# Convolution first stage by partition halves with paired row tiles, and earlier PSUM copies in fc1

## The chip, the cores and the metric

The kernel runs on one core of one Trainium2 chip. The metric is the device time of one execution in microseconds. A core has five engines that run side by side, each with a queue that it works off in order: TensorE (PE, with PEld for its weight loads), VectorE (DVE), ScalarE (ACT), GpSimd (POOL) and SyncE (SP), which here mostly issues DMAs. TensorE writes its results to PSUM, which has eight banks of 512 f32 per partition; DVE and ACT read them from there.

## The reference

One layer of a hybrid block on x of 2048 positions by 1024 channels, in f32:

```python
h = rmsnorm(x, g_mix); p = h @ w_in            # 512 Fourier columns, 3 x 512 Hyena columns
y_f = rmsnorm(fourier_mix(p[:, :512]), g_fourier)
u = short_conv(p[:, 512:], conv_w, conv_b); x1, x2, z = split(u)
for n, gate in enumerate((x1, x2)):            # two long convolutions, by FFT
    y = irfft(rfft(z, 4096) * k_freq[:, n], 4096)[:2048]
    z = gate * (y + z * long_d[n])
x = x + concat(y_f, rmsnorm(z, g_hyena)) @ w_out
x = x + square(relu(rmsnorm(x, g_mlp) @ w_fc1)) @ w_fc2
out = rmsnorm(x, g_final)
```

The two convolutions have 512 channels each; fc1 is 1024 by 4096 and fc2 4096 by 1024.

## The kernel before

The stages follow one another: input projection, short convolution, Fourier mix and filters (to about 618 us of the profiled execution), the two long convolutions (`hyena`, to about 845), output projection (`project_out`), fc1 (about 1045 to 1675) and fc2.

**The convolutions.** `hyena` works in eight blocks: `n` (first or second convolution) by `ct` (four groups of 128 channels). The transform over 4096 points is done in two matmul stages with a turn between them:

- `first(c)` (L712 to L719), for c = 0 to 7, takes 16 channels. Its two matmuls (L718) multiply `zz`, 128 partitions by 16 positions by 16 channels = 256 columns, by the two matrices `e1[:, sp, :]`. The table builds `e1z` so that matrix `sp` is nonzero only in partitions 64 sp to 64 sp + 63: each matmul has 128 rows, of which 64 are zeros. The two results fill the two halves of one PSUM bank, and `turned` (L446) transposes the bank on DVE into `G`.
- `second(q)` (L721 to L735), for q = 0 to 7, does four matmuls of `G` (L725, so it needs all eight turns), then ACT, DVE and POOL multiply by the filter's spectrum.
- `inverse(q)` (L736 to L742) does four matmuls (L741) and an ACT copy into `V`; `turn` transposes `V` into `W` on DVE.
- `gate(q)` (L749 to L757) does two matmuls (L754), each with 64 columns of weights, into the two partition halves of a bank, and DVE multiplies by the gate.

The loop below `blocks` runs block i with q = 0 to 7: `second(q)` of block i, at q = 1 four `gate` of block i - 2, then `inverse`, then `first` of block i + 1 as the table `FIRSTS` says: two at q = 0, two at q = 1, one each at q = 2 to 5. So the first stage of one block is woven into the block before it; only block 0's stands alone, ahead of the loop.

**fc1.** `fc1` multiplies by a Strassen-like scheme: each of the 32 steps does seven products (m1 to m7) of twelve 128x512 matmuls (in mm3, three for each of four slices: high by high, high by low, low by high). Several products add up in one bank `pu`: m1, then m6, then m7, then m4 of the same step. After m1, m6 and m7 the bank's state is copied out by `keep` on ACT (L1142 to L1145; `km1`, `ku2`, `ku3`), and the next product may not add to the bank before that copy is done. A step i issues m1, then m4 and m3 of step i - 1 among its own m2, m6, m5, m7. Tokens are taken in two blocks of 1024: steps 0 to 15 and 16 to 31. In step 15, right after the last use of each product's token operand, the operand of the second block is loaded into the same tile and split into a high part (ACT, L184) and a low part (DVE, L185).

**What sets the order.** Each engine's queue is made by the tile framework when the kernel is built: it takes the instructions by priority, which is their place in the program text, but passes over one that it expects to be still waiting. Under `tc.high_priority(offset=400)` an instruction counts as if it stood 400 places earlier. The framework adds the semaphore waits; two accesses to one bank of a tile are ordered even where their columns differ.

Of the kernel before, what the change touches and what calls it, by code (L numbers as in the profile page):

```python
# [10 lines left out]
F32 = mybir.dt.float32  # L11
# [118 lines left out]
P = 128  # L130
# [6 lines left out]
def hybrid_block(ctx: ExitStack, tc: tile.TileContext, A, out):  # L137
    nc = tc.nc
# [24 lines left out]
    small = ctx.enter_context(tc.tile_pool(name="small", bufs=8))  # L163
# [4 lines left out]
    def pa(nm):  # L168
        return ps.tile([P, 512], F32, tag="a", name=nm, bufs=8)
# [11 lines left out]
    def split(hi, lo, src, scale=None, eng=None):  # L181

        if scale is None:
            nc.scalar.copy(hi, src)  # L184
            (eng or nc.vector).tensor_sub(lo, src, hi)  # L185
        else:
            nc.scalar.mul(hi, src, scale)  # L187
            nc.vector.scalar_tensor_tensor(out=lo, in0=src, scalar=scale, in1=hi, op0=ALU.mult, op1=ALU.subtract)  # L188
# [255 lines left out]
    def turned(dst, c, src):  # L444

        nc.vector.transpose(dst.rearrange("p c f e -> p c e f")[:, 8 * c : 8 * c + 8], src)  # L446
# [230 lines left out]
    def hyena(hp, wp, rp, zz, e1, b1, f2, a2, work):  # L677
# [3 lines left out]
        def big(nm):  # L681
            return (rp if nm == "W" else wp).tile([P, 64, 32, 2], F32, tag=nm, name=nm, bufs=1 if nm == "W" else 2)

        class Block:
# [24 lines left out]
                        nc.gpsimd.memset(ks[h : h + 1, 1, 0, :], 0.0)  # L709
                return ks  # L710

            def first(self, c):  # L712
                if c == 0:
                    self.G = big("G")
                p = pa("pz1")
                lo = 128 * self.ct + 16 * c
                for sp in range(2):
                    nc.tensor.matmul(p[:, 256 * sp : 256 * sp + 256], lhsT=e1[:, sp, :], rhs=zz[:, :, lo : lo + 16], start=True, stop=True)  # L718
                turned(self.G, c, p.rearrange("p (l c e) -> p c e l", c=8, e=2))  # L719

            def second(self, q):  # L721
                ks = self.ahead.pop(q) if q in self.ahead else self.spectrum(q)
# [36 lines left out]
        LAG = 3  # L759
        TURNS = ((0,), (1,), (2, 3), (4, 5), (6, 7))  # L760
        LAST = ((0,), (1, 2), (3, 4), (5, 6), (7,))
        FIRSTS = ((0, 1), (2, 3), (4,), (5,), (6,), (7,), (), ())
        blocks = [Block(n, ct) for n in range(2) for ct in range(4)]
        for k in range(4):
            blocks[0].ahead[k] = blocks[0].spectrum(k)

            nc.sync.dma_start(a2[:, 8 * k : 8 * k + 8], A["a2"][:, 8 * k : 8 * k + 8])
        for c in range(8):
            blocks[0].first(c)
        for i in range(8):  # L770
            cur, old, older, new = (blocks[j] if 0 <= j < 8 else None for j in (i, i - 1, i - 2, i + 1))
            for q in range(8):
# [28 lines left out]
                if new:  # L801
                    for c in FIRSTS[q]:
                        new.first(c)
# [247 lines left out]
    def fc1_load(b, blk, n):  # L1051

        nc.sync.dma_start(b[n][1].bitcast(F32), bd[blk][n])
# [14 lines left out]
    def fc1_sums(eng, wa, wb, s):  # L1068
        a11, a12, a21, a22 = wa[:, 0:4], wa[:, 4:8], wb[:, 0:4], wb[:, 4:8]
        eng.tensor_add(s[0], a21, a22)  # L1070
        eng.tensor_sub(s[1], s[0], a11)
        eng.tensor_sub(s[2], a11, a21)
        eng.tensor_sub(s[3], a12, s[1])
# [16 lines left out]
    def fc1_store(c, queue, f, n):  # L1090
        blk, f = divmod(f, 16)
        queue.dma_start(ad[blk][n][f], c)
# [23 lines left out]
    def fc1(mp, rp, zp, b, first, following, begun):  # L1116


        def weights(wa, wb, step):
            a = {}  # L1120
            a11, a12, a22 = wa[:, 0:4], wa[:, 4:8], wb[:, 4:8]

            def put(n, src, eng=None):
                a[n] = [mp.tile([P, 4, P], FR, tag=f"a{h}", name=f"a{h}{n}", bufs=9) for h in "hl"]
                split(*a[n], src, None, eng)

            if step == 0:
                s = None, None, a11, a12
            else:
                if step > 1:  # L1130
                    put("m1", a11)
                    put("m2", a12, nc.gpsimd)
                s = [mp.tile([P, 4, P], F32, tag="sa", name=f"s{j}", bufs=4) for j in range(4)]
                fc1_sums(nc.gpsimd, wa, wb, s)
                put("m6", s[1])
                put("m5", s[0], nc.gpsimd)
            put("m7", s[2])
            put("m3", s[3], nc.gpsimd)
            put("m4", a22, nc.gpsimd)
            return a  # L1140

        def keep(p, nm):  # L1142
            t = mp.tile([P, 512], F32, tag="keep", name=nm, bufs=4)
            nc.scalar.copy(t, p)  # L1144
            return t  # L1145

        def activate(f, half, h, p, other):
            c = mp.tile([P, 512], F32, tag="c", name="c", bufs=11)
            n = {(0, 0): "m1", (1, 0): "m2", (1, 1): "m4"}.get((half, h))
            fc1_activate(c, p, other, nc.sync if f < 30 else nc.scalar, f, n)  # L1150
            acts[f, half, h] = c

        def sums(f):

            a11, a12, a21, a22 = (acts.pop((f, *k)) for k in ((0, 0), (1, 0), (0, 1), (1, 1)))
            s1, s2, s4 = (mp.tile([P, 512], F32, tag="c", name=n, bufs=11) for n in ("s1", "s2", "s4"))
            nc.vector.tensor_add(s1, a21, a22)
            nc.vector.tensor_sub(s2, s1, a11)
            nc.vector.tensor_sub(a21, a11, a21)
            nc.vector.tensor_sub(s4, a12, s2)  # L1160
            for n, t in (("m6", s2), ("m5", s1), ("m3", s4), ("m7", a21)):
                fc1_store(t, nc.sync if f < 30 else nc.scalar, f, n)

        acts = {}

        mp.tile([P, 512], F32, tag="c", name="c", bufs=11)
        mp.tile([P, 512], F32, tag="keep", name="keep", bufs=4)
        for h in "hl":  # L1170
            mp.tile([P, 4, P], FR, tag=f"a{h}", name=f"a{h}", bufs=9)
        mp.tile([P, 4, P], F32, tag="sa", name="sa", bufs=4)
        b["m4"] = [mp.tile([P, 4, 512], FR, tag=f"b{h}m4", name=f"b{h}m4") for h in "hl"]
        with tc.high_priority(offset=700):
            fc1_load(b, 0, "m4")
            old, nxt = None, weights(*first, 0)
        with tc.high_priority(offset=200):
            for n in ("m7", "m4", "m3"):
                fc1_split(b, n)
        acts[0, 0, 0] = mp.tile([P, 512], F32, tag="c", name="c0", bufs=11)  # L1180
        nc.sync.dma_start(acts[0, 0, 0], ad[0]["m1"][0])
        for i in range(33):
            def use(p, a, n, start, step):
                if n in a:
                    fc1_product(p, a[n], b[n], start)
                if step == 15:
                    fc1_tokens(b, 1, n)

            if i < 32:
                a = nxt  # L1190
                if i < 31:
                    nxt = weights(*(fc1_weights(rp, (i + 1) % 16, 1 - i % 2) if i else following), i + 1)
                pu, pm = (pa("p1u"), pa("p1m")) if i > 1 else begun[3 * i : 3 * i + 2]
                use(pu, a, "m1", True, i)
                if i:
                    m1 = keep(pu, "km1")
            if old:
                use(old["u"], old["a"], "m4", False, i - 1)
                activate(i - 1, 1, 0, old["u"], None)
            if i < 32:  # L1200
                use(pm, a, "m2", True, i)
                if i:
                    activate(i, 0, 0, pm, m1)
            if old:
                use(old["v"], old["a"], "m3", False, i - 1)
                activate(i - 1, 0, 1, old["v"], old["u2"])
                sums(i - 1)
            if i < 32:
                use(pu, a, "m6", False, i)
                with tc.high_priority(offset=0 if i else 400):  # L1210
                    u2 = keep(pu, "ku2")
                pv = pa("p1v") if i else begun[2]
                use(pv, a, "m5", True, i)
                use(pu, a, "m7", False, i)
                u3 = keep(pu, "ku3")
                activate(i, 1, 1, pv, u3)
                old = {"u": pu, "v": pv, "a": a, "u2": u2}

        zf = zp.tile([P, 8, 2, 512], FR, tag="zz", name="zf")
        fc2_begun = {}  # L1220
        for i, n in enumerate(("m1", "m2")):
            parts = []
            for j, v in enumerate(fc2_rows(0, n, 0)):
                t = rp[:, 2 * i + j, :].rearrange("p (f c) -> p f c", f=2)
                nc.sync.dma_start(t, v)
                parts.append((zf[:, 4 * i + 2 * j], zf[:, 4 * i + 2 * j + 1]))
                split(*parts[j], t)
            fc2_begun[n] = [pa("p2" + "um"[i]) for _ in range(4)]
            for j, p in enumerate(fc2_begun[n]):
                fc2_product(p, j, *parts, True)  # L1230
        return fc2_begun
# [205 lines left out]
    zz, = zzs  # L1437
    b1 = load(tabs.enter_context(pool("tabs2", "right")), "b1", [P, P], A["b1"])
    with pool("raws") as rp:
        with pool("wts") as wp:  # L1440
# [7 lines left out]
            with pool("op") as op:  # L1448
                first = project_out(op, work, raws, b)
# [58 lines left out]
```

## Time and profile before

| | us |
|---|---|
| median of 3 runs (2299.31 to 2301.06) | 2300.55 |
| the profiled execution | 2297.96 |
| its span | 2296.2 |
| PE busy, in matmuls | 2237.3 |
| DVE busy | 1509.3 |
| ACT busy | 1110.5 |
| POOL busy | 824.8 |

In the profile, a row of the timeline is start, length, engine, line, operation, out<-in, form, count, and in brackets the idle time before it and what ended it. A count x8 merges eight instructions in a row; the length runs from the first one's start to the last one's end. A matmul's own length includes the time until its result is written, so that lengths of neighbours overlap: what it costs PE is the distance from one start to the next. A row of a tile's list is engine, operation, tile, count, then the shortest, median and longest duration in ns. "f32" also stands for the fp32r operands of mm3 in matmul rows.

### The profile page before, as it was taken

What the parts mean: (1) busy time and instruction counts of PE and PEld (TensorE: products, weight loads), DVE (VectorE), ACT (ScalarE), POOL (GpSimd) and SP (SyncE); (2) the same over time, 40 slices, a digit from 0 to 9 for tenths busy, and PEclk for the clock granted to TensorE, in tenths of its full rate; (3) what the DMA queues carried; (4) which work ended last, traced back from release to release, by engine and by line L of the source; (5) the groups of instructions that cost most, each with busy time, mean ns of one, the idle gap of its engine ahead of it and who ended that gap; (6) DMA issues with size and microseconds to landing.
All of it is one profiled execution on the core that took longest, in us unless ns stands there. A gap on an engine that the chain in (4) does not pass through costs nothing.

```text
span 2296.2 us, 31043 instructions
## 1 busy us (share of the span) xinstructions
PE 2237.3 (97%) x11025; PEld 1853.2 (81%) x11025; DVE 1509.3 (66%) x2258; ACT 1110.5 (48%) x1849; POOL 824.8 (36%) x623
## 2 busy tenths in 40 slices
PE   8999999999899989998999989999999999999998
PEld 6887788799788858887888878888888888888886
DVE  6999776778678774458444465444476666866667
ACT  6555211566366564456555565555543333533333
POOL 3344323677376611146555556555400000000000
PEclk9999999999999999999999999999999999999999
DMA  8545886689987766667444475444489766866631
GB/s 266 181 140 187 329 303 245 226 292 319 324 274 208 216 195 187 178 202 234 158 149 150 150 250 162 152 152 151 142 315 346 245 190 195 299 195 193 192 119 74
DMA packets 298797, 487.31 MB, mean 212 GB/s; under 512 B 17477, under 2 KB 141711, under 8 KB 294417
## 3 DMA queue, kind: packets, MB, share of 16 engines
q1 hardware_dynamic: 292977, 470.91, 62.5%
q10 hardware_dynamic: 5664, 14.41, 1.8%
q8 instruction: 87, 1.43, 0.3%
q14 instruction: 69, 0.57, 0.1%
HBM read 314.64 MB, written 169.05 MB: 211 GB/s over the span
## 4 chain that ended last, share of the span: by engine, by line
PE 78%; DVE 4%; DMA 3%; ACT 2%; issue 1%; POOL 1%; SPq 0%; ACTq 0%; DVEq 0%; POOLq 0%
PE p2u L193 5%; PE p2u L192 5%; PE p2u L194 5%; PE p1u L192 5%; PE p1u L194 5%; PE p1u L193 5%; PE p2v L193 3%; PE p2v L192 3%; PE p2v L194 3%; PE pu L194 2%; PE pu L193 2%; PE pu L192 2%; PE p1v L192 2%; PE p1v L194 2%; PE p1v L193 2%; PE po L192 2%
## 5 line engine op out<-in xcount | busy, mean ns | idle before, releaser
L184 ACT CAST qahm<-ra 128x1024 fp32r<-128x1024 f32 x110 | 115.9, 1053 | 344.5 <-PE p2u L193 172.0
L185 DVE TENSOR_TENSOR qalm<-ra,qahm 128x1024 fp32r<-128x1024 f32 x110 | 134.7, 1225 | 153.8 <-ACT qahm L184 151.8
L1282 POOL TENSOR_TENSOR acc<-acc,gfin 128x512 f32<-128x512 f32 x4 | 5.1, 1276 | 631.9 <-DMA out<-acc 624.7
L192 PE MATMUL pu<-wh,xh 128*128 128x512 f32 x512 | 204.4, 400 | 4.8 <-ACT wh L187 3.6
L193 PE MATMUL pu<-wl,xh 128*128 128x512 f32 x512 | 201.7, 394 | 3.6 <-DVE wl L188 3.5
L194 PE MATMUL pu<-wh,xl 128*128 128x512 f32 x512 | 201.2, 393 | 0.2 <-DVE xl L185 0.2
L193 PE MATMUL p2u<-qblm,qahm 128*128 128x512 f32 x504 | 196.1, 389 | 0.0
L192 PE MATMUL p2u<-qbhm,qahm 128*128 128x512 f32 x504 | 195.8, 389 | 0.0
L194 PE MATMUL p2u<-qbhm,qalm 128*128 128x512 f32 x504 | 195.8, 389 | 0.0
L185 DVE TENSOR_TENSOR qblm<-rb,qbhm 128x1024 fp32r<-128x1024 f32 x110 | 134.1, 1219 | 3.5 <-ACT qbhm L184 3.0
L383 POOL TENSOR_TENSOR acc<-acc,cw 128x512 f32<-128x512 f32 x45 | 59.9, 1331 | 201.6 <-DVE acc L360 200.3
L184 ACT CAST ahm<-s 128x512 fp32r<-128x512 f32 x124 | 76.6, 621 | 100.6 <-PE p1v L193 55.3
L185 POOL TENSOR_TENSOR alm<-W,ahm 128x512 fp32r<-128x512 f32 x63 | 85.5, 1357 | 99.7 <-ACT ahm L184 93.1
L193 PEld LDWEIGHTS pu<-wl,xh 128*128 128x128 f32 x512 | 97.3, 190 | 25.6 <-DVE wl L188 4.9
L184 ACT CAST qbhm<-rb 128x1024 fp32r<-128x1024 f32 x110 | 115.3, 1048 | 5.4 <-DMA rb<-in_w_fc 4.2
L192 PEld LDWEIGHTS pu<-wh,xh 128*128 128x128 f32 x512 | 97.1, 190 | 25.7 <-ACT wh L187 4.0
L194 PEld LDWEIGHTS pu<-wh,xl 128*128 128x128 f32 x512 | 97.2, 190 | 21.3 <-DVE xl L185 1.1
L192 PEld LDWEIGHTS p2u<-qbhm,qahm 128*128 128x128 f32 x504 | 94.6, 188 | 20.2 <-issue 0.3
L193 PEld LDWEIGHTS p2u<-qblm,qahm 128*128 128x128 f32 x504 | 94.6, 188 | 19.6
L194 PEld LDWEIGHTS p2u<-qbhm,qalm 128*128 128x128 f32 x504 | 94.6, 188 | 19.5
L192 PE MATMUL p1u<-bm,ahm 128*128 128x512 f32 x252 | 100.2, 398 | 8.1 <-ACT ku L1144 8.1
L184 ACT CAST ahm<-W 128x512 fp32r<-128x512 f32 x94 | 57.5, 615 | 100.9 <-PE p1u L193 98.8
(397 smaller groups left out, 6429.5 us busy)
## 6 DMA issues: line engine op xcount, KB each, us to landing
W<-in_w_fc SPq DMA_DIRECT2D x66, 512.0 KB
spec<-ks SPq DMA_DIRECT2D x32, 1024.0 KB
ks<-spec SPq DMA_DIRECT2D x64, 512.0 KB
rb<-td SPq DMA_DIRECT2D x64, 512.0 KB
ra<-a1m SPq DMA_DIRECT2D x56, 512.0 KB
ra<-a0m SPq DMA_DIRECT2D x54, 512.0 KB
rb<-in_w_fc SPq DMA_DIRECT2D x46, 512.0 KB
f<-in_w_fc SPq DMA_DIRECT2D x16, 1024.0 KB
```

The source lines that it names most:

```text
L184: nc.scalar.copy(hi, src)
L185: (eng or nc.vector).tensor_sub(lo, src, hi)
L192: nc.tensor.matmul(o, lhsT=lh, rhs=rh, start=start, stop=False, skip_group_check=more)
L193: nc.tensor.matmul(o, lhsT=lh, rhs=rl, start=False, stop=False, skip_group_check=more)
L194: nc.tensor.matmul(o, lhsT=ll, rhs=rh, start=False, stop=stop, skip_group_check=more)
L383: nc.gpsimd.tensor_add(m1, m1, cw[:, 3, :])
L1282: nc.gpsimd.tensor_mul(acc[i][:, c], acc[i][:, c], gfin[:, c])
```

## The change

`first` takes a step s = 0 to 8 in place of a channel group. In step s it multiplies partitions 0 to 63 of group s by the nonzero half of the first matrix into a new bank, then partitions 64 to 127 of group s - 1 by that of the second into the other half of the bank that step s - 1 opened, and then turns group s - 1. Between the two matmuls of one bank stands a new ACT copy of one column of it into a small tile that nobody reads; by the framework's rule for banks, the second matmul waits for it. `FIRSTS` gains step 8 at q = 6, and the lone run ahead of the loop has nine steps.

In fc1, `keep` gets the step and gives its copy the priority offset of 400 in steps 0, 15, 16 and 17, for all of `km1`, `ku2` and `ku3`; before, only `ku2` of step 0 had it.

```diff
-            def first(self, c):
-                if c == 0:
-                    self.G = big("G")
-                p = pa("pz1")
-                lo = 128 * self.ct + 16 * c
-                for sp in range(2):
-                    nc.tensor.matmul(p[:, 256 * sp : 256 * sp + 256], lhsT=e1[:, sp, :], rhs=zz[:, :, lo : lo + 16], start=True, stop=True)
-                turned(self.G, c, p.rearrange("p (l c e) -> p c e l", c=8, e=2))
+            def first(self, s):
+
+                if s == 0:
+                    self.G, self.z1 = big("G"), {}
+                for sp, c in ((0, s), (1, s - 1)):
+                    if not 0 <= c < 8:
+                        continue
+                    p = pa("pz1") if sp == 0 else self.z1[c]
+                    h, lo = slice(64 * sp, 64 * sp + 64), 128 * self.ct + 16 * c
+                    nc.tensor.matmul(p[:, 256 * sp : 256 * sp + 256], lhsT=e1[h, sp, :], rhs=zz[h, :, lo : lo + 16], start=True, stop=True)
+                    if sp == 0:
+                        self.z1[c] = p
+
+                        nc.scalar.copy(small.tile([P, 1], F32, tag="ssq", name="z1"), p[:, 0:1])
+                if s:
+                    turned(self.G, s - 1, self.z1.pop(s - 1).rearrange("p (l c e) -> p c e l", c=8, e=2))
...
-        FIRSTS = ((0, 1), (2, 3), (4,), (5,), (6,), (7,), (), ())
+        FIRSTS = ((0, 1), (2, 3), (4,), (5,), (6,), (7,), (8,), ())
...
-        for c in range(8):
-            blocks[0].first(c)
+        for s in range(9):
+            blocks[0].first(s)
...
-        def keep(p, nm):
+        def keep(p, nm, i):
             t = mp.tile([P, 512], F32, tag="keep", name=nm, bufs=4)
-            nc.scalar.copy(t, p)
+
+            with tc.high_priority(offset=400 if i in (0, 15, 16, 17) else 0):
+                nc.scalar.copy(t, p)
             return t
...
-                    m1 = keep(pu, "km1")
+                    m1 = keep(pu, "km1", i)
...
-                with tc.high_priority(offset=0 if i else 400):
-                    u2 = keep(pu, "ku2")
+                u2 = keep(pu, "ku2", i)
...
-                u3 = keep(pu, "ku3")
+                u3 = keep(pu, "ku3", i)
```

## The prediction

> **What bounds the kernel now.** I read the page's busy shares first, then the windows over the convolutions' blocks, then PE's list of waits, then the timelines of the two places that the diff touches.
>
> ```profile
> span 2296.2 us, 31043 instructions
> ...
> PE 2237.3 (97%) x11025; PEld 1853.2 (81%) x11025; DVE 1509.3 (66%) x2258; ACT 1110.5 (48%) x1849; POOL 824.8 (36%) x623
> ```
> ```profile
> 626.00:646.00 20.00, 19.09 (x136) 17.76 (x136) 9.04 (x15) 9.14 (x16) 12.52 (x12) 1.00 1.06 363
> ...
> 722.20:747.20 25.00, 25.00 (x178) 21.50 (x177) 20.36 (x34) 14.64 (x25) 16.36 (x15) 1.00 0.73 213
> ```
> ```profile
> PE p1u L192 <- ACT ku L1144: 8.1, 4, 3.7
> ```
>
> TensorE is the bound almost everywhere. In the windows (length, then busy time of PE, PEld, DVE, ACT, POOL) a convolution block of 25.00 us has PE busy for all 25.00, with DVE at 20.36: each nanosecond added to or taken from PE's queue there is added to or taken from the time. Only the first block has slack, 0.91 us. In the list of waits, PE's largest single loss is 8.1 us in four waits of fc1 for the PSUM copy `ku`. So the change has two terms: what it does to PE's queue in the blocks, and what becomes of these waits.
>
> **Term 1: the first stage by halves.** A_c is the half of channel group c on partitions 0 to 63, B_c the half on 64 to 127. First the price of a matmul, of two that run side by side, and of entering and leaving a tiled form; `gate` (L754) already uses one, by column halves.
>
> ```profile
> L718 PEld LDWEIGHTS pz<-zz,e1z x256: 187/190/192, 618.0 to 789.6; 128*128 128x128 f32 x128
> L718 PE MATMUL pz<-zz,e1z x256: 377/379/382, 618.1 to 789.9; 128*128 128x256 f32 x128
> ```
> ```profile
> L754 PEld LDWEIGHTS pb<-W,b x112: 132/133/137, 673.2 to 843.5; 128*64 128x64 f32 x112
> ```
> ```profile
> 672.21 1.05 PE L725 MATMUL pz<-G,f2h 128*128 128x128 f32 x8
> 673.19 3.66 PE L754 MATMUL pb<-W,b 128*64 128x512 f32 x16
> 676.78 1.16 PE L741 MATMUL pv<-y,f 128*128 128x128 f32 x8
> 677.78 1.89 PE L718 MATMUL pz<-zz,e1z 128*128 128x256 f32 x8
> 679.51 1.06 PE L725 MATMUL pz<-G,f2h 128*128 128x128 f32 x8
> 680.40 1.05 PE L741 MATMUL pv<-y,f 128*128 128x128 f32 x8
> ```
> ```profile
> 835.01 1.94 PE L754 MATMUL pb<-W,b 128*64 128x512 f32 x8 [0.73 <-DVE W L446]
> ```
>
> The trace holds two instructions for each f32 matmul. Eight of L718 take 679.51 - 677.78 = 1.73 us, 0.216 each, so one half costs 0.43 and one call of `first` 0.865; a result is there 0.379 - 0.216 = 0.16 after its stream. In `gate`, sixteen instructions of twice the columns take 3.66 and eight take 1.94: 1.72 for eight more is 0.215 each, what L718 pays for half the columns. So the two column halves of `gate` run side by side, two instructions in each 0.43. I take the same for row halves: an A and a B together cost 0.43.
>
> The switch: L725 before `gate` has eight at the pace 680.40 - 679.51 = 0.89, so `gate` was due at 673.10 and began at 673.19: 0.09. From 673.19 to 676.78 are 3.59 us against eight pairs of 0.43 = 3.44: 0.15. L741 behind it takes 677.78 - 676.78 = 1.00, not 0.89: 0.11. In and out cost 0.35. Row halves load 128 columns of weights where `gate` loads 64; the loads' medians differ by 0.190 - 0.133 = 0.06. I take **0.40 for a switch in and out**. Lowest bound: only the 0.09 on each side, 0.18, if loads hide. Upper: 0.50, if the two weight loads go one after the other.
>
> The Trainium skill's page "TensorEngine Tiling (Array Packing)", Theoretical Speedup, gives up to 2x for 64 rows, and its Key Properties say that a change of mode drains the array. By the first alone, the eleven slots counted below cost 4.7 us instead of 6.9, and term 1 would be 7 x -2.2 = -15; the 0.35 at `gate` shows the drain to be as large as most of what a pair saves, so I do not take it.
>
> Now a block. It has seven visits (q = 0 to 6) to the first stage, before 2, 2, 1, 1, 1, 1, 0 calls, after 2, 2, 1, 1, 1, 1, 1:
> - q = 2 to 5, A_c beside B_c-1: 0.43 + 0.40 = 0.83 against 0.865. **-0.04 each, -0.16.** The copy that B waits for was made a visit earlier.
> - q = 6, B_7 alone: nothing before, now **+0.83**.
> - q = 0: A_0, A_1, B_0. B_0 waits for ACT's copy of A_0. q = 1: A_2 beside B_1, A_3, B_2, which waits for the copy of A_2. In both, three slots, 1.29, plus a switch: 1.69 against 1.73, if no wait shows.
>
> The wait is on PE's queue, and behind it stand `second` of the next q and everything after; ACT's queue decides:
>
> ```profile
> 694.98 0.60 ACT L728 ACTIVATE zs<-pz 64x512 f32<-64x512 f32 x1
> 695.47 1.89 PE L718 MATMUL pz<-zz,e1z 128*128 128x256 f32 x8
> ...
> 696.19 0.61 ACT L742 COPY V<-pv 128x512 f32<-128x512 f32 x1
> ...
> 697.20 1.05 PE L725 MATMUL pz<-G,f2h 128*128 128x128 f32 x8
> ```
> ```profile
> 677.98 0.65 ACT L742 COPY V<-pv 128x512 f32<-128x512 f32 x1 [3.49 <-PE pv L741]
> ```
> ```profile
> 600.32 0.40 ACT L567 ACTIVATE diag<-ident,both 128x128 f32<-128x128 f32 x1
> ...
> 600.92 0.30 PEld L580 LDWEIGHTS pdiag<-diag,ones 128*128 128x128 f32 x2 [0.22 <-ACT diag L567]
> ...
> 601.44 0.27 ACT L581 COPY norms<-pdiag 128x128 f32<-128x128 f32 x1 [0.16 <-PE pdiag L580]
> ```
>
> A one-column copy isn't in the trace; the nearest is 0.27 (128 columns out of PSUM), and PE starts 0.20 after ACT's end (600.72 to 600.92). At q = 0 ACT is free at 696.80, so B_0 starts at 697.27, ends at 697.70, and with 0.2 to leave the form PE is at 697.90 instead of 697.20: +0.70. If the framework's order puts matmuls of `second` into that wait, there is a second switch instead: 3 x 0.43 + 2 x 0.40 = 2.09, +0.36. It does so where it foresees a wait (two matmuls of the next product stand ahead of the waiting one at 1350.94, below), so I take **+0.36**. At q = 1: A_2 done 677.98 + 0.43 + 0.16 = 678.57, ACT free 678.63, copy and release to 679.10, B_2 and the way out to 679.73 against 679.51: **+0.22** (up to 0.36).
>
> Per block: 0.36 + 0.22 - 0.16 + 0.83 = +1.25; seven blocks, 8.75; the first block's 0.91 idle hides about as much: **+7.8**. Bounds: without any wait showing, 2 x -0.04 - 0.16 + 0.83 = +0.59 per block, 3.2 in all; with q = 0 at 0.70 and q = 1 at 0.36, +1.73, about 11. The opening run of `first` (nine steps) I cost at nothing: there DVE's eight transposes are the chain, and they start later but run closer. If that cover is gone it costs one copy's round trip, 0.6. The copies themselves, 8 x 0.27 = 2.2 us a block, lie on ACT, which has 14.64 of 25 busy; and a PSUM bank is held one visit longer, which I cost at nothing with eight banks and no wait for one among PE's waits.
>
> The last transpose moves from q = 5 to behind B_7:
>
> ```profile
> 691.90 1.06 PE L725 MATMUL pz<-G,f2h 128*128 128x128 f32 x8
> 692.27 1.30 DVE L446 STREAM_TRANSPOSE W<-V 128x512 f32<-128x512 f32 x2
> ...
> 693.68 1.06 PE L725 MATMUL pz<-G,f2h 128*128 128x128 f32 x8
> ```
>
> B_7 would end near 692.5, DVE is free at 693.57, one transpose is 0.65: done at 694.2, plus 0.2 is 694.4. The next block's `second`, 693.68 before, comes at 694.5. Hidden, by a tenth; without that cover up to 0.65 per block, 4.6.
>
> **Term 2: fc1's copies.**
>
> ```profile
> 1350.94 0.40 PE L192 MATMUL p1u<-zf,ahm 128*128 128x512 f32 x1
> ...
> 1353.01 0.58 ACT L1144 COPY ku<-p1u 128x512 f32<-128x512 f32 x1
> ...
> 1353.64 0.49 PE L192 MATMUL p1u<-bm,ahm 128*128 128x512 f32 x1 [2.06 <-ACT ku L1144]
> ```
> ```profile
> 1370.09 0.39 PE L192 MATMUL p1v<-bm,ahm 128*128 128x512 f32 x1
> ...
> 1370.68 2.36 DVE L185 TENSOR_TENSOR bm<-bm 128x1024 fp32r<-128x1024 f32 x2 [0.26 <-ACT bm L184]
> ...
> 1372.81 0.40 PE L192 MATMUL p1u<-zf,ahm 128*128 128x512 f32 x1
> ...
> 1376.29 0.56 ACT L1144 COPY ku<-p1u 128x512 f32<-128x512 f32 x1
> ...
> 1376.91 0.80 PE L192 MATMUL p1u<-bm,ahm 128*128 128x512 f32 x1 [3.70 <-ACT ku L1144]
> ...
> 1382.19 0.63 PE L193 MATMUL p1u<-zf,ahm 128*128 128x512 f32 x1
> ```
> ```profile
> 1378.00:1382.00 4.00, 4.00 (x11) 3.13 (x10) 3.96 (x3) 1.79 (x2) 3.59 (x3) 0.50 0.55 136
> ```
>
> Steps 15 and 16 hold two of the four waits: m7 may not write the bank until `ku2` is copied, and ACT makes that copy behind casts of the next tokens. The product m6 that it copies was done before m5 began, a product (1372.81 - 1370.09 = 2.72) earlier, so a copy that goes first removes 2.06 and 3.70. After the longer wait the granted clock is 0.50 (last row), and the twelve matmuls from 1376.91 to 1382.19 take 5.28 instead of 2.72: 2.56 more. Together 8.3. What is late next: with 2.06 gained, m7 of step 16 is due at 1370.75, but the low parts of its tokens come from DVE between 1370.68 and 1373.04; half of that time, 1.2, shows as a wait, and I allow 0.2 for later tokens. The casts that now stand behind a copy slip by 0.58; m7's wait already contains that. The other two waits (steps 0 and 1) aren't touched: `ku2` of step 0 had the priority before, and for step 0 only `ku3` is new, which nothing waited for. **-6.9**, between -8.3 and -2.1 (only the first wait goes). PE is dense from there to the end, so it is kept.
>
> **Sum.** +7.8 - 6.9 = +0.9. The profiled execution is 2297.96 us (span 2296.2 and 1.76 around it), 2.59 under the median 2300.55; it becomes 2298.9, the median **2301.5**.
>
> **The rivals.**
> - *A and B don't run side by side* (slower). Each visit issues A's two instructions and then B's two. If PE keeps that order, B's first starts with A's second, and a pair takes three streams of 0.216 instead of two: +0.216 for five pairs a block, 7.6 in all, **2309**. It decides at the first pair of q = 2. Against it: `gate` has the same order, and its sixteen would take nine slots of 0.43 = 3.87 and the 0.16 behind the last, 4.03, not 3.66. The Trainium skill's page "TensorE: Matmul & The Clock Gate", Part 3, The mechanism, states this rule (matmuls start and end strictly in program order); at `gate` the trace disagrees. Chance 0.12; wholly serial, +15, **2317**, 0.04.
> - *Waits on the path* (slower): q = 0 pays 0.70, and the last transpose shows with 0.65. +1.0 per block, 7, **2308.5**. For: margins of a tenth; against: the block itself gets longer. 0.13.
> - *A cheaper switch* (faster): 0.18 instead of 0.40 on eight switches a block is -1.76, seven blocks -12, **2289**; half of it, **2295**. Against: `gate`, with a smaller load, pays 0.35. 0.12.
> - *Fc1's second wait stays*, as a wait for tokens, or because the copy isn't moved past the casts: -2.1 instead of -6.9, **2306**. For: the tokens' DVE work ends at 1373.04 and 1.2 is shown already. 0.09.
>
> **How the numbers follow.** The forecast has 0.50. What a measurement can tell from no change is 0.2%, 4.6 us. Within it lies most of the forecast and half of the fc1 rival: 0.42. Slower: the first two rivals, the rest of the fc1 rival and the forecast's upper edge (11 in term 1): 0.36. Faster: the cheaper switch, and the forecast's lower edge (3.2 - 8.3 = -5): 0.22. The range leaves out the wholly serial case and the larger half of the cheap switch: 2294 to 2312; the forecast alone, 2297 to 2306.
>
> **What would show it.** Right: L718 in visits of some 0.83 with both halves' instructions starting together, a visit behind q = 6, the blocks at about 26.2 us with PE dense, and waits for the small copy at q = 0 and 1; in fc1, no wait over 1.5 us for `ku` near 1353 and 1377, and the clock at 1.00 there. Wrong: blocks of 25 us or less, blocks above 27, or a wait of PE for tokens in fc1 as long as the one that left.

## The result and the profile after

The changed kernel takes 2319.26 us (median of four runs, 2316.93 to 2320.18) against 2300.81 of the kernel before on the same chip: ratio 1.0074, 95% interval 1.0055 to 1.0093, 18 us slower. The prediction was 2301.5 with a range of 2294 to 2312; the time lies above it. One execution of all those below, the third of e12 at 2655.66 us, was in a slower state of the chip and is left out of the times.

The page's first lines:

```profile
span 2317.8 us, 31115 instructions
...
PE 2252.1 (97%) x11025; PEld 1842.6 (79%) x11025; DVE 1510.3 (65%) x2258; ACT 1114.9 (48%) x1913; POOL 823.4 (36%) x623
```

The span is 21.6 us longer. 3.6 of that are there ahead of any changed instruction (the last product of the kernel's spectrum starts at 621.62 instead of 618.03): the profiled execution of before was a quick one, 2297.96 us against a median of 2302.24 in 23 later runs on another chip, and in two later kernels with unchanged convolutions (e2 and e8 below) block 0 starts 1.8 and 2.0 us later than in it. In `hyena` the blocks stand as follows (windows from the first `second` of a block to that of the next: length, busy time of PE, PEld, DVE, ACT, POOL, granted clock, DMA share, GB/s). After, blocks 0 to 3:

```profile
629.22:660.79 31.57, 26.22 (x137) 20.54 (x138) 11.96 (x18) 12.69 (x30) 14.74 (x15) 0.68 0.90 286
660.79:684.04 23.25, 22.48 (x162) 18.22 (x161) 17.23 (x29) 15.91 (x35) 15.94 (x15) 1.00 0.75 227
684.04:710.21 26.17, 26.16 (x176) 19.42 (x176) 20.23 (x33) 14.67 (x33) 16.08 (x14) 1.00 0.69 201
710.21:736.78 26.57, 26.20 (x177) 19.43 (x177) 20.19 (x33) 15.70 (x34) 15.72 (x14) 1.00 0.68 199
```

Before, blocks 0, 1 and 3:

```profile
626.02:646.54 20.52, 19.23 (x137) 17.76 (x137) 9.58 (x16) 9.14 (x16) 12.96 (x12) 1.00 1.05 360
646.54:668.39 21.85, 21.56 (x160) 20.49 (x161) 16.11 (x26) 15.70 (x28) 15.54 (x15) 1.00 0.86 261
693.68:718.67 24.99, 24.99 (x178) 21.47 (x177) 20.28 (x33) 14.61 (x26) 16.60 (x15) 1.00 0.72 212
```

Block 0 lost 31.57 - 20.52 = 11.05 us, blocks 1 to 6 lost 0.9 to 1.6 each, 7.9 in all. In block 0, PE's idle time grew from 20.52 - 19.23 = 1.29 to 31.57 - 26.22 = 5.35, and its busy time by 6.99 while the clock fell to a mean of 0.68: a wait, and matmuls at half speed around it. PE's list of waits names the wait, and shows that those for `ku` are still there (8.1 before):

```profile
PE p1u L192 <- ACT ku L1154: 7.0, 4, 2.8
PE pz L721 <- ACT z L725: 5.4, 1, 5.4
```

The timeline of ACT, with the row of PE that waited, at block 0 after:

```profile
623.61 1.07 ACT L603 COPY ks<-pk 128x512 f32<-128x512 f32 x2
...
625.53 1.07 ACT L603 COPY ks<-pk 128x512 f32<-128x512 f32 x2
...
636.91 0.29 ACT L707 COPY ks<-ks 1x128 f32<-1x128 f32 x1 [9.36 <-DMA ks<-spec]
637.23 0.59 ACT L736 ACTIVATE zs<-pz 64x512 f32<-64x512 f32 x1
637.83 0.58 ACT L737 COPY zs<-pz 64x512 f32<-64x512 f32 x1
638.43 0.22 ACT L725 COPY z<-pz 128x1 f32<-128x1 f32 x2
...
638.65 1.22 PE L721 MATMUL pz<-zz,e1z 64*128 64x256 f32 x2 [5.35 <-ACT z L725]
```

and of ACT before:

```profile
618.36 1.07 ACT L603 COPY ks<-pk 128x512 f32<-128x512 f32 x2 [1.23 <-PE pk L600]
...
630.91 0.29 ACT L707 COPY ks<-ks 1x128 f32<-1x128 f32 x1 [11.48 <-DMA ks<-spec]
```

The new copies (`z`, L725) of block 1's A_0 and A_1 take 0.22 us for two. But they stand in ACT's queue behind the copy of the first row of block 0's spectrum (L707), and that one waits for a load from memory. Before, ACT waited there 11.48 us and PE did not care; now PE's B_0 hangs on it. The load itself is late too: `z` copies of the opening run stand between the last copies of the kernel's spectrum (L603), the last pair of these ends 626.60 - 618.36 - 1.07 = 7.2 us later than before (3.6 of it from upstream), and the store, the load and L707 come after it.

The later blocks, by PE's timeline. After, block 2 (the rows of `second`, and the new visit at q = 6):

```profile
684.04 1.16 PE L733 MATMUL pz<-G,f2h 128*128 128x128 f32 x8 [0.63 <-DVE G L446]
...
687.78 1.16 PE L733 MATMUL pz<-G,f2h 128*128 128x128 f32 x8
...
695.12 1.16 PE L733 MATMUL pz<-G,f2h 128*128 128x128 f32 x8
...
697.74 1.16 PE L733 MATMUL pz<-G,f2h 128*128 128x128 f32 x8
...
705.58 1.16 PE L733 MATMUL pz<-G,f2h 128*128 128x128 f32 x8
...
707.56 0.70 PE L721 MATMUL pz<-zz,e1z 64*128 64x256 f32 x2
708.19 1.16 PE L733 MATMUL pz<-G,f2h 128*128 128x128 f32 x8
...
710.21 0.38 PE L733 MATMUL pz<-G,f2h 128*128 128x128 f32 x1
```

Before, block 3 from q = 2 on:

```profile
704.50 1.06 PE L725 MATMUL pz<-G,f2h 128*128 128x128 f32 x8
...
707.15 1.06 PE L725 MATMUL pz<-G,f2h 128*128 128x128 f32 x8
...
715.10 1.05 PE L725 MATMUL pz<-G,f2h 128*128 128x128 f32 x8
...
716.89 1.06 PE L725 MATMUL pz<-G,f2h 128*128 128x128 f32 x8
718.67 0.72 PE L725 MATMUL pz<-G,f2h 128*128 128x128 f32 x5
```

The distances from one `second` to the next give the price of each visit (before, q = 0 and 1 begin at 693.68 and 697.20; the range at q = 7 is that of blocks 2 to 6):

| q | before | after | difference | forecast |
|---|---|---|---|---|
| 0 | 3.52 | 3.74 | +0.22 | +0.36 |
| 1 | 7.30 | 7.34 | +0.04 | +0.22 |
| 2 to 5, each | 2.65 | 2.62 | -0.03 | -0.04 |
| 6 | 1.79 | 2.61 | +0.82 | +0.83 |
| 7 | 1.78 | 2.02 to 2.49 | +0.24 to 0.71 | 0 |

### The profile page after: what moved, and what is told of

It reads as the page before. It is cut to its first block, busy times and chain, and to the rows that moved or that the text cites. A ratio compares the mean times of both kernels' runs of the same rounds, so it can differ in the third digit from the quotient of the medians.

```text
span 2317.8 us, 31115 instructions
## 1 busy us (share of the span) xinstructions
PE 2252.1 (97%) x11025; PEld 1842.6 (79%) x11025; DVE 1510.3 (65%) x2258; ACT 1114.9 (48%) x1913; POOL 823.4 (36%) x623
## 4 chain that ended last, share of the span: by engine, by line
PE 79%; ACT 3%; DVE 3%; DMA 2%; POOL 1%; issue 1%; SPq 0%; ACTq 0%; POOLq 0%; DVEq 0%
PE p2u L192 5%; PE p2u L193 5%; PE p2u L194 5%; PE p1u L192 5%; PE p1u L194 5%; PE p1u L193 4%; PE p2v L192 3%; PE p2v L194 3%; PE p2v L193 3%; PE pu L194 2%; PE pu L193 2%; PE pu L192 2%; PE pk L532 2%; PE pz L733 2%; PE p1v L192 2%; PE p1v L194 2%
## 5 line engine op out<-in xcount | busy, mean ns | idle before, releaser
L185 DVE TENSOR_TENSOR qalm<-ra,qahm 128x1024 fp32r<-128x1024 f32 x110 | 134.6, 1224 | 156.1 <-ACT qahm L184 152.1
L185 DVE TENSOR_TENSOR qblm<-rb,qbhm 128x1024 fp32r<-128x1024 f32 x110 | 134.0, 1218 | 1.2 <-ACT qbhm L184 1.0
L185 POOL TENSOR_TENSOR alm<-W,ahm 128x512 fp32r<-128x512 f32 x63 | 86.6, 1375 | 97.2 <-ACT ahm L184 97.2
L740 POOL TENSOR_TENSOR zs<-zs,ks 128x512 f32<-128x512 f32 x64 | 83.3, 1302 | 65.1 <-ACT zs L737 56.6
```

The costliest lines, as they stand in the source:

```text
L740: nc.gpsimd.tensor_mul(zs, zs, ks[:, 1])
```

## The experiments

Twelve kernels, each timed against the kernel before on the same chip. The table gives the ratio with its 95% interval and, from the profile, the time from block 0's first `second` to block 7's (before: 793.64 - 626.02 = 167.62; the two kernels below with unchanged convolutions have 167.72 and 169.52; after 186.57).

| kernel | ratio | blocks 0 to 6 |
|---|---|---|
| e1, convolutions' part alone | 1.0070 [1.0058, 1.0083] | 186.52 |
| e2, fc1's part alone | 0.9995 [0.9986, 1.0003] | 167.72 |
| e3, e1 with z copies on DVE in the opening run | 1.0053 [1.0040, 1.0066] | 178.38 |
| e4, e1 with a whole-row opening run | 1.0054 [1.0041, 1.0067] | 180.38 |
| e5, e1 with block 0's L707 on POOL | 1.0066 [1.0053, 1.0080] | 185.73 |
| e6, e4 with block 0's L707 on POOL | 1.0059 [1.0046, 1.0072] | 180.93 |
| e10, e6 with block 1's L707 on POOL too | 1.0037 [1.0024, 1.0051] | 178.61 |
| e12, half rows in blocks 3 to 7 only | 1.0037 [1.0023, 1.0051] | 176.69 |
| e7, B two groups behind A, five visits | 1.0017 [1.0008, 1.0025] | 171.37 |
| e11, e7's form in blocks 3 to 7 only | 1.0005 [0.9996, 1.0014] | 166.78 |
| e9, three visits, blocks 3 to 7 only | 1.0038 [1.0024, 1.0051] | 179.21 |
| e8, fc1's ku2 alone, steps 15 and 16 | 1.0001 [0.9993, 1.0010] | 169.52 |

**Which part costs what.** e1 is the changed kernel with fc1 as before, e2 the kernel before with the new `keep`.

> The convolutions' part alone; fc1's copies as before. My theory after the result: the convolutions lose all of the time and a bit more (about +10.8 us in the opening run and block 0, +1.2 a block in the six that follow, the rest behind them), and fc1's part gives back only about 0.9: 2320 us, +17 to +21 against before. The prediction's sum has +7.8 here: 2308.6. Rival: fc1's part does bring its 6.9, and the convolutions cost 25: 2326.

> The fc1 part alone; convolutions as before. My theory: the wait that goes (2.06) comes back in pieces at steps 0, 1 and 16, so about -0.9 (2299 to 2301.5 us), with waits for ku of some 7 us in all. The prediction's step and the rival: -6.9, 2294 us, waits for ku of about 2.4 us.

The convolutions lose everything: 2318.28 against 2302.30, +16.0 us (1 us under the range of my theory). Fc1's part brings 0.7 us at the median; its interval (0.9986 to 1.0003, -3.2 to +0.7 us) holds no change, but not a gain of 6.9. The waits for `ku` in e2 sum to 6.1, not to 2.4.

**Block 0: the opening run.** Two ways to take the `z` copies out from between the spectrum's copies:

```diff
-  nc.scalar.copy(z1, p[:, 0:1])                       # e3
+  (nc.vector.tensor_copy if self is blocks[0] else nc.scalar.copy)(z1, p[:, 0:1])
...
-  for s in range(9): blocks[0].first(s)               # e4
+  for c in range(8): blocks[0].rows(c)                # first(c) of the kernel before
```

> The convolutions' part alone, but in the opening run the one-column copy between A and B is made by DVE and not by ACT, so that nothing new stands in ACT's queue ahead of the last copies of the kernel's spectrum; the half-row matmuls stay. My theory (the order of ACT's queue delays the last spectrum store, its load, the copy of its first row and the z copies behind that): the wait of 5.35 us at block 0 is gone, the granted clock is 1.00 from 628 to 648, time about 10 us under the convolutions' part alone (2309 to 2311). Rival (the half-row matmuls themselves let the clock fall): the wait is gone but the clock is 0.50 for some 15 us behind the opening run, 2314 to 2317. Second rival (DVE, which makes the transposes there, becomes the chain): clock at 1.00 and the opening run some 2 us longer, 2312.

> The convolutions' part alone, but block 0's first stage in the opening run is whole rows as before; blocks 1 to 7 by halves. My theory: no copy in ACT's queue ahead of the spectrum copies, so block 0 starts as before; about 10 us under the convolutions' part alone (2309 to 2311), clock 1.00. The rival with half rows and the clock gives the same here, and differs from the kernel with the copy on DVE. Third rival (the wait comes from block 0's own visits, whose copies stand behind the copy of the spectrum's first row in any order): the wait at block 0 stays at 3 us or more, 2316 to 2320.

Both come to the same time, 2314.61 and 2314.93, some 3.5 us under e1 (the intervals just overlap); 10 were expected. In e3 the wait for `z` at block 0 is down to 0.5, but the copies on DVE delay the transposes: a wait of 4.0 for G ends the opening run, and the clock falls in it. In e4 everything up to block 0 is as before, and PE still waits:

```profile
PE pz L730 <- ACT z L734: 4.6, 1, 4.6
```

So the third rival holds in kind (its 2316 to 2320 was 1 us too slow): the visits in block 0 make a wait by themselves, and the opening run only adds to it. The rival that half rows themselves lower the clock has e3's time (2314 to 2317) but isn't borne out: e5, below, has the opening run by halves and keeps a clock of 1.00 from 624 to 650, while e4, with whole rows there, is at 0.50 from 635.4 to 642.2, from 3 us into the wait on.

**Block 0: the copy that waits for the load.** L707 for block 0, or 0 and 1, goes to POOL:

```diff
-  nc.scalar.copy(ks[64:65, 0, 0, :], ks[64:65, 1, 0, :])
+  (nc.gpsimd.tensor_copy if self is blocks[0] else nc.scalar.copy)(ks[64:65, 0, 0, :], ks[64:65, 1, 0, :])
```

> The convolutions' part alone, with block 0's copy of the spectrum's first row (L707) on POOL and not on ACT; the opening run by halves, with its z copies on ACT. My theory: PE waits at block 0 because the z copies of block 1's A_0 and A_1 stand in ACT's queue behind that copy, which waits for a load. So PE's wait for z (4.6 to 7.0 us in the three kernels that have it) is gone, and since the spectrum itself still lands late, some 2 us of wait for y come at the first inverse product: about 4 us under the convolutions' part alone, +11 to +13 against before. Rival (the order in the opening run alone makes the wait): z still waits 4 us or more, +16.

> As the kernel with the whole-row opening run, and with block 0's copy of the spectrum's first row on POOL. My theory: both causes at block 0 are gone, and what is left is the price of the visits, +1.25 a block, as the prediction's first term has it: +7 to +9 against before, 2309 to 2311, granted clock 1.00 from 628 on, PE's waits in block 0 under 1.5 us. Rival (the wait only moves to the product y, which needs the same load): +11 to +13.

The wait for `z` is gone in both (two of 0.40 are left), which shows that L707 made it. The time stays: 2317.55 and 2316.08, +15.3 and +13.8. So my theory of the time falls in both; e6's rival (+11 to +13) comes nearer in size, but not in place, for little moved to y. The wait moved to the end of block 0, as 4.3 and 5.5 us for G, and the clock falls to 0.50 there instead (in e6 from 652.1 to 659.0). e6, ACT, DVE and PEld there:

```profile
652.73 0.29 ACT L707 COPY ks<-ks 1x128 f32<-1x128 f32 x1 [6.68 <-POOL ks L709]
653.04 0.59 ACT L745 ACTIVATE zs<-pz 64x512 f32<-64x512 f32 x1
...
654.26 0.69 DVE L748 TENSOR_TENSOR y<-pz,ks 128x512 f32<-128x512 f32 x1 [3.59 <-ACT zs L746]
...
654.87 0.71 DVE L446 STREAM_TRANSPOSE G<-pz 128x512 f32<-128x512 f32 x1
...
655.63 1.15 PEld L742 LDWEIGHTS pz<-G,f2h 128*128 128x128 f32 x5 [5.64 <-DVE G L446]
```

The last transpose, which the change moved from q = 5 to q = 6, stands on DVE behind a product y; y waits for ACT's zs, zs stands behind block 1's L707, and that one waits for block 1's load (POOL's memset L709 ahead of it waits for the same load). The test of this chain is to free block 1's copy as well:

> As the kernel with the whole-row opening run and block 0's first row on POOL, but the first row of block 1's spectrum is copied on POOL too. There the wait at block 0 had moved to its end: 5.45 us for G, since the last transpose stands on DVE behind a product y that waits for ACT's zs, which stands behind the copy of block 1's first row, which waits for a load. My theory: with that copy off ACT the last transpose is made some 4 to 5 us earlier, block 0 takes about 22 us, and the time is about 4 under that kernel, +8 to +10 against before. Rival (the loads themselves set block 0): the wait moves once more, to y, and the time stays at +13.

Block 0 of e6 and of e10 (columns as above):

```profile
629.47:655.63 26.16, 19.91 (x136) 15.64 (x137) 12.00 (x17) 12.42 (x29) 14.86 (x16) 0.93 1.03 341
```
```profile
630.77:653.76 22.99, 19.91 (x136) 15.64 (x136) 12.00 (x17) 13.15 (x29) 13.24 (x14) 1.00 1.04 350
```

Block 0 takes 22.99 (about 22 in the theory), G is waited for 2.29 instead of 5.45, the clock stays at 1.00, and the time is +8.4 us, within the theory's range. The intervals of e6 and e10 overlap, as those of e1 and e4 do; those of e1 and e10 don't. The three steps together (whole rows in the opening run, and two copies of a first row off ACT) bring +16.0 down to +8.4, which is about the price of the visits in seven blocks (8.75 in the prediction).

**The visits alone.** Half rows only where the loads are far ahead, and other arrangements of the visits there:

```diff
+  ROWS = ((0, 1), (2, 3), (4,), (5,), (6,), (7,), (), ())
-  for c in FIRSTS[q]: new.first(c)
+  for c in (FIRSTS if i > 1 else ROWS)[q]: (new.first if i > 1 else new.rows)(c)
...
-  for sp, c in ((0, s), (1, s - 1)):                  # e7, e9, e11
+  for sp, c in ((0, s), (1, s - 2)):
-  FIRSTS = ((0, 1), (2, 3), (4,), (5,), (6,), (7,), (8,), ())
+  FIRSTS = ((), (0, 1), (2, 3), (4, 5), (6, 7), (8, 9), (), ())      # e7, e11
+  FIRSTS = ((), (), (0, 1, 2), (3, 4, 5), (6, 7, 8, 9), (), (), ())  # e9
```

> The change's half rows (B one group behind A, seven visits) only for blocks 3 to 7, whose first stage stands in the stretches of blocks 2 to 6; the opening run and blocks 1 and 2 by whole rows as before; fc1 as before. My theory: the price of the visits alone, without what happens in block 0: 5 x 1.25 = +6.2 us against before, 2308.5, with blocks 2 to 6 at 26.2 us (25.0 before) and block 0 at 20.5 to 21.7 as before. Rival (block 0's loss comes back elsewhere, because the loads of the spectrum that follow are late): over +9.

> As the kernel with the whole-row opening run and the first row on POOL, but B follows A by two channel groups and not by one, in five visits of two groups (q = 1 to 5: A0 A1; A2 B0 A3 B1; A4 B2 A5 B3; A6 B4 A7 B5; B6 B7). No B waits for a copy in its own visit, and the form is entered five times a block instead of seven (eight, if a wait is filled). By the prediction's prices: 10 x 0.43 + 5 x 0.40 = 6.3 us a block against 6.92 for whole rows: -0.6 a block, -4 in all, 2298. If a switch costs 0.18 only: -12, 2290. Rival (the transposes come later and in pairs, so that the next block's second stage waits for DVE, or a PSUM bank is waited for): blocks above 25 us and waits for G of over 0.5 us a block, 2304 or more.

> Half rows only for blocks 3 to 7, B two groups behind A, five visits of two groups. By the prediction's prices 10 x 0.43 + 5 x 0.40 = 6.3 against 6.92: -0.6 a block, as the kernel with five visits in all blocks showed (24.4 against 25.0): -3 us, 2299. Rival (a wait for G or for a bank in some blocks): 0 to +2.

> Half rows only for blocks 3 to 7, B two groups behind A, three visits (A0 A1 A2 B0; A3 B1 A4 B2 A5 B3; A6 B4 A7 B5 B6 B7) at q = 2, 3, 4. By the prediction's prices 10 x 0.43 + 3 x 0.40 = 5.5 against 6.92: -1.4 a block, -7 us, 2295, if no wait shows. Some B stands only two slots (0.86) behind its A in the same visit; with ACT in an operation of 0.6 the copy comes late by up to 0.5, twice a block: -2 to -4 us, 2299. Rival (the transposes come in a bunch on DVE and the banks of the next products are late): 0 or slower, 2302 to 2308.

e12: blocks 0 and 1 are as before (20.76, 21.88), blocks 3 to 6 take 26.13 to 26.34, the price of the visits. But the time is +9.0 us (2309.7), not +6.2, about the size of its rival: block 2, the first whose stretch has half rows, takes 29.25 against 25.29. There ACT stands idle for 2.08 ahead of L707, no later than before (2.16 at 667.31, at no cost); nine operations follow it without a gap, the z copies come behind them, PE waits 1.50, and then the clock falls:

```profile
677.00:679.00 2.00, 1.26 (x5) 0.93 (x6) 1.90 (x4) 0.73 (x4) 1.27 (x1) 0.84 0.86 246
679.00:681.00 2.00, 2.00 (x9) 1.45 (x10) 1.12 (x2) 0.52 (x1) 1.27 (x1) 0.50 0.74 201
```

e7 and e11, whose copies have a whole visit to arrive and whose form is entered five times, show undisturbed blocks of 24.37 us. In e11:

```profile
747.87:772.24 24.37, 24.37 (x179) 19.18 (x178) 21.16 (x34) 15.55 (x34) 15.74 (x15) 1.00 0.74 217
```

That is 0.62 under the 24.99 of whole rows, where 10 x 0.43 + 5 x 0.40 against 6.92 gave 0.6: the prices of a pair and of a switch hold. The kernels are no faster for it. e7 loses it in blocks 0 and 1 (23.89 and 24.83 against 20.52 and 21.85) and takes +3.6, the size of its rival; e11 loses it in one block of 26.25 with a wait of 1.14 for z and one of 25.09 with 0.46: 2302.76 against 2300.76, no difference that can be measured, and again the size of its rival. e9 is slower still, 2310.43, above even its rival: its last three blocks with half rows take 25.5 and not 23.6, its first two 31.47 and 27.69, and PE's list has

```profile
PE pz L730 <- ACT z L734: 7.3, 5, 3.7
```

The longest of the five:

```profile
691.49 0.19 POOL L709 MEMSET ks<- 1x128 f32 x1 [5.58 <-DMA ks<-spec]
691.58 0.29 ACT L707 COPY ks<-ks 1x128 f32<-1x128 f32 x1 [3.88 <-issue]
...
691.90 0.16 ACT L734 COPY z<-pz 128x1 f32<-128x1 f32 x1
...
692.11 0.79 PE L730 MATMUL pz<-zz,e1z 64*128 64x256 f32 x1 [3.66 <-ACT z L734]
```

It isn't the two slots between A and B that make these waits: the copy stands behind the next block's L707, which waits for its load (released with L709, which waits for the same), as in block 0. The same holds for all five in e9 and for the waits for z that cost e7 and e11 their gain (e7 2.32 at 675.46 behind an L707 at 674.93; e11 1.14 at 694.11 behind one at 693.58). In e9's last three blocks such a wait is 0.70 to 0.87 of the 1.9 us a block; the rest is not settled. L707 off ACT in all blocks, with five visits, is the version that this points to, and no run has it. None of the arrangements that were run is faster than the kernel before.

**fc1.** ku2 of steps 15 and 16 alone, with a larger offset:

```diff
-  with tc.high_priority(offset=0 if i else 400):
+  with tc.high_priority(offset={0: 400, 15: 1500, 16: 1500}.get(i, 0)):
       u2 = keep(pu, "ku2")
```

> The kernel before, with only ku2 of steps 15 and 16 moved up, at a priority offset of 1500; steps 0 and 17, km1 and ku3 as before. The copy of step 16 lands at the same place in ACT's queue as with the offset of 400. My theory: the wait of 2.06 at step 15 goes and the one of step 16 falls from 3.70 to 2.8, without what the offset costs at steps 0 and 1: -3 to -4 us, 2299. Rival (the prediction's step): both waits and the clock come back, -7, 2295. Second rival (the change at steps 15 and 16 is worth nothing, since PE then waits for tokens): -0.5, 2302.

The second rival holds in size: 2302.30 against 2302.24. The wait of 2.06 is gone. But the product behind m7 on the same bank now waits 1.91 for ku3; PE comes that much later to step 16, where its wait is down to 0.67, and a later product waits 2.96 for DVE's c. Together that is 5.54, where 5.76 had been:

```profile
PE p1v L192 <- DVE c L1080: 3.0, 1, 3.0
```

The windows of e8 ahead of that wait show why (columns as above):

```profile
1384.00:1388.00 4.00, 3.93 (x18) 2.90 (x17) 4.00 (x3) 2.23 (x5) 3.92 (x3) 1.00 0.39 136
1388.00:1392.00 4.00, 3.09 (x14) 2.15 (x12) 4.00 (x3) 0.00 (x0) 4.00 (x3) 1.00 0.43 116
```

DVE and POOL are full, and ACT, after 2.23 us of work, is idle: DVE works off the sums of activations (L1158 to L1160) and low parts (L185) ahead of c. So once the copies come early the time seems to go to DVE at the token change; no run took work off DVE to show it.

## Why the prediction was wrong, step by step

**PE-bound blocks; a pair costs 0.43, a switch 0.40: right.** The table by q and the 24.37 of e7 and e11 bear both out. A pair's two matmuls start within 0.01 us of each other (697.10 and 697.11 at q = 2 of block 2), so the rival "not side by side" is out; the measured prices leave no room for the "cheaper switch". Whether A's two instructions stand in PE's queue ahead of B's, as the first rival took for granted, the trace doesn't show, so neither this pair nor `gate` tells whether PE departs from the order of its queue.

**+1.25 a block: right in sum, not in its parts.** 7.9 over six blocks is 1.3. The waits at q = 0 and 1 cost less (+0.26 against +0.58). PE's order stayed as written, and ACT's one-column copy takes 0.16, where 0.27 was taken. Of the 0.24 to 0.71 at q = 7, 0.10 is the first product behind the visit at q = 6 (708.19 to 709.19 against 0.90 before); the rest is the last transpose, costed as hidden "by a tenth": the margin was smaller than the queue in front of it. That the sum came out is in part luck: the waits cost less and the transpose more.

**"The first block's 0.91 idle hides about as much": this step failed.** Block 0 was to take 0.34 more (1.25 less the 0.91) and took 11.05 more. The prediction knew that "ACT's queue decides" and looked at it in a steady block only, where it is short; for the rest it went by ACT's busy share, 14.64 of 25. In block 0 ACT had been the engine that waits: 11.48 us on a load, in the row of before shown above, which cost PE nothing then. A new wait of PE for ACT makes all that ACT waits for PE's own. e5, e6 and e10 show the chain: the wait goes when L707 leaves ACT, turns up at the last transpose, and shrinks when the next L707 leaves as well.

**"The opening run I cost at nothing": wrong, by some 3.4 us.** The run itself is no longer (7.39 from its first matmul to the first `second`, 7.88 before), as forecast. But the copies stand between those of the spectrum, so that the last store to memory is issued at 626.63 instead of 619.46, and the loads behind it wait. The step looked at DVE's chain and not at who else uses ACT's queue. e4, which takes the halves out of the opening run, is 3.4 us under e1 at the median, with intervals that just overlap.

**The clock.** It isn't in term 1 at all, though the prediction had it in fc1. Of block 0's 11.05, 4.06 are idle time; the visits account for 0.68 (PE's busy time in e10's block 0, at a clock of 1.00, is 19.91 against 19.23), and the other 6.3 are matmuls at half clock.

**Fc1: -6.9 forecast, -0.7 measured.** Another step that failed here is "a copy that goes first removes 2.06 and 3.70". The changed kernel at step 16, ACT and PE:

```profile
1392.23 2.00 ACT L184 CAST bm<-bm 128x1024 fp32r<-128x1024 f32 x2
...
1394.13 0.62 ACT L184 CAST ahm<-s 128x512 fp32r<-128x512 f32 x1
...
1395.85 1.03 ACT L184 CAST bhm<-blm 128x1024 fp32r<-128x1024 f32 x1
...
1396.78 0.58 ACT L1154 COPY ku<-p1u 128x512 f32<-128x512 f32 x1
...
1397.41 0.80 PE L192 MATMUL p1u<-bm,ahm 128*128 128x512 f32 x1 [2.84 <-ACT ku L1154]
```

ku2 is still behind four casts: the wait fell from 3.70 to 2.84, and the clock is at 0.50 behind it again (from 1396.9 to 1400.3; in e2 from 1377.4 to 1384.2, as long as before). With an offset of 1500 the copy lands in the same place, so it is not the rank that holds it. The wait at step 15 went, but m4 behind it waits 0.60 for ku3 (0.97 in e2). In this execution the waits at steps 0 and 1 also grew by 1.2, and one of 1.88 for DVE's c came in at 1412.00; e2, with the same fc1, has 2.28 against 2.31 and 0.35 there, so these two aren't shown to come from the change. This is the prediction's own rival "fc1's second wait stays", above all because "the copy isn't moved past the casts"; it had 0.09 and deserved more. e8 suggests that work on DVE would have kept most of the time even with an earlier copy.

**Range.** Forecast and result differ by some 18 us: block 0 by 10.7 (the opening run's share is in it), fc1 by 6, the rest is small. The rivals on the slow side were each priced for steady blocks, and none for the block whose data is still on its way.

## What to carry to other kernels

Before PE is made to wait for an engine, read that engine's whole queue, above all in the first iterations, and look for the instruction that waits for a load: its idle time, free so far, becomes PE's. A saved half of a matmul must pay for the entry into the tiled form and for the slots that a stagger adds; count slots and entries, and put several groups in one visit. And a copy given a higher priority gains nothing while it stays behind the same work, nor more than the next wait in line leaves.

## What the runs showed of the hardware

The granted clock fell to 0.50 in PE's long waits, 3.7 us after their start in e1, 3.4 in e5, 3.1 in e4, 2.4 in e3 and 2.0 in e6. The Trainium skill's page "TensorE: Matmul & The Clock Gate", Part 1, What's actually happening, puts the fall behind an idle window of about 3.4 us; e1 and e5 agree with it, and the others fell sooner. Shorter waits do not fit it at all: e12's wait of 1.50 ended at 677.74 and the clock was 0.50 from 678.4 to 681.8, while 2.29 us in e10 left it at 1.00. And in the changed kernel it fell at 629, with no more than a wait of 0.92 there:

```profile
628.00:630.00 2.00, 1.08 (x5) 0.78 (x4) 1.16 (x2) 0.00 (x0) 0.00 (x0) 0.72 1.03 397
630.00:634.00 4.00, 3.29 (x11) 2.16 (x9) 0.00 (x0) 0.00 (x0) 0.00 (x0) 0.50 1.00 276
```

e1 and e5, with the same opening run and a wait of 0.9, kept 1.00 there. What made it fall in that execution stays open. The traces' records of the clock show one thing more: in the convolutions each stretch at 0.50 lasted a multiple of 3.41 us (3.41 in e12, 6.83 in e4 and e6, 10.24 in e3 and e5, 13.65 in e1, 20.48 in the changed kernel), so that the cost of a wait goes in steps and differs between executions of like waits.
